# Zeroing the pairs that are not allowed on GpSimd instead of masking the scores on TensorE

## The chip, the cores and the metric

The kernel runs on one core of one Trainium2 chip. The metric is the time of one execution on the device, in microseconds (us), as the median of several runs. Beside it stands one profiled execution, whose trace gives the start and the length of every instruction. The engines are named as in the profile: PE is TensorE (matmuls; PEld its weight loads), DVE is VectorE, ACT is ScalarE, POOL is GpSimd, SP is the queue from which most loads are issued.

## The reference, cut to what matters

The input x has 256 rows of 4096 numbers in float32. The reference normalizes the rows, multiplies them by a 4096 x 16384 matrix, which gives q, k, v and a gate for 32 heads of width 128, runs a stick-breaking attention in each head, multiplies its output by silu(gate) and by a 4096 x 4096 matrix, adds x and normalizes again. What the change touches is the attention of one head:

```python
causal = s_pos[None, :] < t_pos[:, None]
z = jnp.einsum('bhqd,bhkd->bhqk', qb, k, preferred_element_type=jnp.float32) * scale
log_fail = jnp.where(causal, jax.nn.log_sigmoid(-z), 0.0)
suffix = lax.cumsum(log_fail, axis=3, reverse=True) - log_fail
log_a = jax.nn.log_sigmoid(z) + suffix
a = jnp.where(causal, jnp.exp(jnp.where(causal, log_a, 0.0)), 0.0)
return jnp.einsum('bhqk,bhkd->bhqd', a.astype(v.dtype), v)
```

A pair of a query t and a key s is allowed where s < t. Pairs that are not allowed must count nothing in the sum over keys (log_fail is 0) and have no weight (a is 0).

## The kernel before, in words

**The products.** The two big matrices are worked off as 20 units: units 0 to 15 make the projections (two heads each), units 16 to 19 the output. A unit has 16 steps along the 4096 rows of the matrix. The matrix is float32; each tile of it is split by ScalarE into a rounded high part (the casts `wh<-raw`) and by VectorE into the rest (the subtractions `wl<-raw,wh`), and x is split likewise. One product is three matmuls: high by high, high by low, low by high (`mm3`, L813). In units 1 to 15 ten of the 16 steps save one product of eight by sums of blocks: seven products, for which VectorE makes three sums (`sums`, L423) and GpSimd issues two loads that add to what a tile holds (`add_block`, L400). A unit has thus 10 x 7 + 6 x 8 = 118 products. Loads go from SP's queue into 7 buffers `raw`; there are 7 buffers of high parts and 5 of low parts, and TensorE's products follow in a fixed order.

**The order of the work.** `Plan` (L113) lays out the program before it runs. Each piece of work asks for an engine with a cost and a due time; the planner simulates the engines, gives an engine that is free the piece that is due first (`turn`, L229), and emits the instructions in the order of this simulation. Each engine then works off its own list in that order and waits on semaphores where data are not there yet. Costs are formulas by columns (L101 to L110); behind its end a result counts as seen after a tail that depends on the engine: 190 ns for TensorE, 114 for VectorE, 125 for ScalarE, 50 for GpSimd (L122). The issue of a load counts 550 ns on GpSimd (L354). TensorE's pieces of a head (`ten`, L345) ask 400 ns after their input is seen and then go ahead of the next product. Buffers are places in rings (`take`, `give`): `gh` has 4 places and holds the heads' tiles, `att` has one, a bank of PSUM.

**A head.** When a unit's sums are in PSUM, `combine` (L709) puts them together on VectorE and ScalarE into `qk_sb` and `gv_sb`, `gate` (L796) works out silu of the gate, and the two heads follow one after the other while TensorE is in the next unit. `head` (L824) is one chain:

1. TensorE turns q and k (tile `tr`); ScalarE copies them to `qkT`.
2. `scores` (L847): TensorE makes z, 128 keys by 3 x 128 columns. The first 128 columns are the later keys with the later queries, the next 128 the earlier keys with the earlier queries, the last 128 the earlier keys with the later queries. Only the first two squares, the diagonal ones, hold pairs that are not allowed. A third product adds to both squares: an identity (`ident_b`) by a square `off` that holds -3e38 where the key is not before the query, and 0 elsewhere.
3. ScalarE makes ln(1 + exp(-|z|)) in f (L860), VectorE adds max(z, 0) (L867): the softplus. Where z is -3e38 it is 0.
4. ScalarE rounds f to `fh` (L872), VectorE takes the rest `fl` (L873).
5. `scan` (L879): TensorE subtracts from z the sums of f over the keys from each key on, as products with a triangle of -1, and turns the gate's first half.
6. `weights_of` (L897): ScalarE makes a = exp(-relu(-z)). Where z is -3e38 it is 0.
7. `out_of_head` (L909): TensorE multiplies a by v into o and turns the gate's second half; VectorE multiplies o by the gate into `gated`, which GpSimd's queue moves to DRAM at the end of the unit's heads.

The constants come from the start (L619 to L638): GpSimd fills and cuts the triangle and the square `off_f` with affine_select, which keeps an element or replaces it by a fill value, as a linear function of row and column says; VectorE casts them in `constants` (L701). Every instruction that the planner emits has the line L132 in the profile, that of its helper, so the groups are told apart by their tiles.

Of the kernel before, what the change touches and what calls it, by code (L numbers as in the profile page):

```python
# [10 lines left out]
F32 = mybir.dt.float32  # L11
F32R = mybir.dt.float32r
BF16 = mybir.dt.bfloat16
AF = mybir.ActivationFunctionType
ALU = mybir.AluOpType
# [4 lines left out]
P = 128  # L20
# [32 lines left out]
ROWS = 4  # L53
# [47 lines left out]
def vector_ns(n):  # L101
    return 67 + 1.0417 * n


def scalar_ns(n):
    return 98 + n / 1.2


def tensor_ns(n):
    return 0.4167 * n + 8.5 if n > 128 else 109.0  # L110
# [138 lines left out]
def kernel(  # L249
# [10 lines left out]
    nc = Plan(tc)  # L260
# [3 lines left out]
    wp = ctx.enter_context(tc.tile_pool(name="weights", bufs=1))  # L264
# [5 lines left out]
    ap = rooms.enter_context(tc.tile_pool(name="attention", bufs=1))  # L270
# [4 lines left out]
    def minus(out_, full, part):  # L275
        nc.vector.tensor_tensor(out=out_, in0=full, in1=part.bitcast(F32), op=ALU.subtract)
# [34 lines left out]
    for g, (n, k) in enumerate(order):  # L311
        p = parts[n]
        b = p["u"], p["prods"][k][0]
# [12 lines left out]
    def soon(c=4.0):  # L326
        return nc.here + 1e3 * c


    def dve(emit, n, key=None, more=0, **kw):  # L330
        n = n if isinstance(n, tuple) else (n,)
        cost = sum(vector_ns(m) for m in n) + 122 * (len(n) - 1) + more
        return nc.work("vector", cost, emit, soon() if key is None else key, **kw)

    def act(emit, n, key=None, **kw):
        n = n if isinstance(n, tuple) else (n,)
        cost = sum(scalar_ns(m) for m in n) + 100 * (len(n) - 1)
        return nc.work("scalar", cost, emit, soon() if key is None else key, **kw)


    FULL_P, FULL_S = (P,) * 2, (W,) * 2
# [3 lines left out]
    def ten(emit, *n):  # L345
        def others():
            nonlocal since_others
            since_others = 0
            emit()

        return nc.work("tensor", 40 + sum(tensor_ns(m) for m in n), others, nc.here - 1e4, wait=400)
# [262 lines left out]
    for k in range(WARM):  # L614
# [4 lines left out]
    ident = ap.tile([P, P], F32, name="ident")  # L619
    make_identity(tc.nc, ident)  # L620

    nc.rings["gh"][1] += 1
    squares_f = wp.tile([P, 2, P], F32, tag="gh", name="squares_f", bufs=ROWS)
    tri_f, off_f = squares_f[:, 0, :], squares_f[:, 1:2, :]
    nc.gpsimd.memset(tri_f, -1.0)
    nc.gpsimd.affine_select(
        out=tri_f, in_=tri_f, compare_op=ALU.is_ge, fill=0.0, base=0, pattern=[[-1, P]], channel_multiplier=1,
    )

    nc.gpsimd.memset(off_f, -3e38)  # L630
    nc.gpsimd.affine_select(
        out=off_f, in_=off_f, compare_op=ALU.is_ge, fill=0.0, base=0,
        pattern=[[0, 1], [-1, P]], channel_multiplier=1,
    )
    off = ap.tile([P, 1, P], BF16, name="off")
    ident_b = ap.tile([P, P], BF16, name="ident_b")
    neg_tri = ap.tile([P, P], F32R, name="neg_tri")
    neg_one = neg_tri[:, 0:1].broadcast_to([P, P])  # L638

# [61 lines left out]
    def constants():  # L701
        yield nc.until(("used", 0, 1))
        yield dve(lambda: nc.vector.tensor_copy(neg_tri, tri_f), P)
        yield dve(lambda: nc.vector.tensor_copy(off, off_f), P)
        yield dve(lambda: nc.vector.tensor_copy(ident_b, ident), P)
        nc.give("gh")


# [110 lines left out]


    BW = 3 * P
    not_before = off.broadcast_to([P, 2, P])

    def head(u, i):  # L824
        yield nc.take("att", "gh", sooner=True)
        tr = att.tile([P, 2, S], F32, tag="att", name=f"tr{u}_{i}")

        def turn():
            for k in range(2):
                for t in range(NT):  # L830
                    c = k * CW + i * P
                    nc.tensor.transpose(tr[:, k, t * P : (t + 1) * P], st["qk", u][:, t, c : c + P], ident)

        yield ten(turn, P, P, P, P)
        if i == HG - 1:
            nc.give("one")
        qk = wp.tile([P, 2, S], F32, tag="gh", name=f"qkT{u}_{i}", bufs=ROWS)
        yield act(lambda: nc.scalar.copy(qk, tr), 2 * S)
        nc.give("att")
        yield nc.take("att", sooner=True)  # L840
        bank = att.tile([P, W], F32, tag="att", name=f"z{u}_{i}")
        z, gT = bank[:, 0:BW], bank[:, BW:W]

        def turned(to, t):
            nc.tensor.transpose(to, st["gv", u][:, t, i * P : (i + 1) * P], ident)

        def scores():  # L847
            kw = dict(stop=False, skip_group_check=True)
            nc.tensor.matmul(z[:, 0:P], qk[:, 1, P:S], qk[:, 0, P:S], start=True, **kw)
            nc.tensor.matmul(z[:, P:BW], qk[:, 1, 0:P], qk[:, 0, :], start=False, **kw)  # L850
            diagonal = z[:, 0 : 2 * P].rearrange("p (a b) -> p a b", a=2)
            nc.tensor.matmul(diagonal, ident_b, not_before, start=False, **kw)

        yield ten(scores, *FULL_P, *FULL_S, 2 * P)
        nc.give("gh")
        yield nc.take("gh", sooner=True)

        f = wp.tile([P, BW], F32, tag="gh", name=f"f{u}_{i}", bufs=ROWS)

        def soft():  # L860
            nc.scalar.activation(f, z, AF.Abs, scale=scale)
            nc.scalar.activation(f, f, AF.Exp, scale=-1.0)
            nc.scalar.activation(f, f, AF.Ln, bias=1.0)
            nc.scalar.activation(f, f, AF.Copy, scale=1.0 / scale)

        yield act(soft, (BW,) * 4)
        yield dve(  # L867
            lambda: nc.vector.scalar_tensor_tensor(out=f, in0=z, scalar=0.0, in1=f, op0=ALU.max, op1=ALU.add), BW
        )
        yield nc.take("gh", "gh", sooner=True)  # L870
        fh, fl = (wp.tile([P, BW], F32R, tag="gh", name=f"f{k}{u}_{i}", bufs=ROWS) for k in "hl")
        yield act(lambda: nc.scalar.copy(fh, f), BW)  # L872
        yield dve(lambda: minus(fl, f, fh), BW)  # L873
        nc.give("gh")

        if i == 0:
            yield nc.until(("gate", u))

        def scan():  # L879
            kw = dict(start=False, skip_group_check=True)  # L880
            nc.tensor.matmul(z, neg_tri, fh, stop=False, **kw)
            nc.tensor.matmul(z, neg_tri, fl, stop=False, **kw)
            nc.tensor.matmul(z[:, 2 * P : BW], neg_one, fh[:, 0:P], stop=False, **kw)
            nc.tensor.matmul(z[:, 2 * P : BW], neg_one, fl[:, 0:P], stop=True, **kw)
            turned(gT, 0)

        yield ten(scan, BW, BW, P, P, P)
        nc.give("gh", "gh")
        if i == 0:
            yield nc.take("gh", sooner=True)  # L890
            st["o", u] = wp.tile([P, 4, P], F32, tag="gh", name=f"gated{u}", bufs=ROWS)
        gated = st["o", u][:, 2 * i : 2 * i + 2, :].rearrange("p a b -> p (a b)")
        yield nc.take("gh", sooner=True)
        a = wp.tile([P, BW], F32, tag="gh", name=f"a{u}_{i}", bufs=ROWS)


        def weights_of():  # L897
            nc.scalar.activation(a, z, AF.Relu, scale=-scale)
            nc.scalar.activation(a, a, AF.Exp, scale=-1.0)

        yield act(weights_of, (BW, BW))
        yield act(lambda: nc.scalar.copy(gated[:, 0:P], gT), P)
        nc.give("att")
        yield nc.take("att", sooner=True)
        bank2 = att.tile([P, BW], F32, tag="att", name=f"o{u}_{i}")
        o, gT2 = bank2[:, 0:S], bank2[:, S:BW]
        v = lambda t: st["gv", u][:, t, CW + i * P : CW + (i + 1) * P]

        def out_of_head():  # L909
            kw = dict(skip_group_check=True)  # L910
            nc.tensor.matmul(o, v(0), a[:, P:BW], start=True, stop=False, **kw)
            nc.tensor.matmul(o[:, P:S], v(1), a[:, 0:P], start=False, stop=True, **kw)
            turned(gT2, 1)

        yield ten(out_of_head, *FULL_P, *FULL_S, P)
        nc.give("gh")
        if i == HG - 1:
            nc.give("two")
        yield act(lambda: nc.scalar.copy(gated[:, P:S], gT2), P)
        yield dve(lambda: nc.vector.tensor_tensor(out=gated, in0=o, in1=gated, op=ALU.mult), S)  # L920
        nc.give("att")
# [332 lines left out]
    def products():  # L1254
        for g, (n, k) in enumerate(order):
# [18 lines left out]
            nc.here = g * PRODUCT  # L1274

    together(split(KT, "w", HIGHS), split(1, "s", SINGLES), products(), x_stats(), x_factor(), constants())

    def in_turn(works):
# [55 lines left out]
```

## Time and profile before

| What | us |
|---|---|
| median of 3 runs | 1699.45 |
| lowest and highest | 1698.41, 1699.90 |
| the profiled execution's own time | 1698.9 |
| its span, from the first to the last instruction | 1697.1 |
| mean granted TensorE clock, as a share of full speed | 0.997 |
| VectorE: all 128x1024 low parts `wl<-raw,wh`, 813 of 1.22 us | 974.4 |
| GpSimd: 300 issues of adding loads of `w_in` | 258.3 |

The span leaves out what lies before the first and behind the last instruction, 1.8 us here. Busy times of different engines lie beside each other and do not add up. A row of a group gives the engine, the operation, the tile that it writes and those that it reads, the shapes, the count, the busy time, the mean length of one in ns, and the idle time of the engine just before it with what ended it. A row of a timeline gives start and length in us; rows of like instructions that follow each other are one row with a count (x2).

### The profile page before, as it was taken

The numbers are of one execution on the slowest core, as the hardware profiler recorded it, in microseconds if no ns is written. First come the engines' busy times: TensorE is split into PE (matmuls) and PEld (weight loads), VectorE is DVE, ScalarE is ACT, GpSimd is POOL, SyncE is SP. The second block draws the span as 40 slices with busy tenths as digits, with TensorE's granted clock in tenths as the row PEclk, the third lists the DMA queues.
The fourth block names the chain that finished last, engine by engine and source line by source line (L and its number), as shares of the span: only waits on it lengthen the run. The fifth ranks groups of instructions, "written<-read, shape, count | busy, mean of one in ns | idle before, by whom it ended". The sixth has DMA issues, their size and how long they took to land.

```text
span 1697.1 us, 25128 instructions
## 1 busy us (share of the span) xinstructions
PE 1680.2 (99%) x7776; PEld 1417.4 (84%) x7776; DVE 1602.0 (94%) x2025; ACT 1206.7 (71%) x1665; POOL 324.9 (19%) x400
## 2 busy tenths in 40 slices
PE   9999999999999999999999999999999999999997
PEld 7888888888888888888888888888888888888885
DVE  8899999999999999999999999999999978999997
ACT  8986767676767676767676767676868775656654
POOL 0012222121222222222212121212122111212110
PEclk9999999999999999999999999999999999999998
DMA  9978888878787878797978797979797978888895
GB/s 343 332 197 247 232 247 222 252 217 253 215 256 212 256 212 266 199 272 196 276 201 269 198 268 196 272 198 269 204 264 210 300 230 266 245 245 256 246 304 185
DMA packets 248438, 412.77 MB, mean 243 GB/s; under 512 B 28016, under 2 KB 72560, under 8 KB 248304
## 3 DMA queue, kind: packets, MB, share of 16 engines
q1 hardware_dynamic: 194544, 354.24, 62.7%
q0 software_dynamic: 53472, 56.65, 20.0%
q8 instruction: 61, 1.00, 0.2%
q14 instruction: 73, 0.60, 0.1%
q10 hardware_dynamic: 288, 0.28, 0.1%
HBM read 402.93 MB, written 8.13 MB: 242 GB/s over the span
## 4 chain that ended last, share of the span: by engine, by line
PE 94%; DVE 3%; DMA 1%; issue 1%; ACT 1%; SPq 0%; DVEq 0%; ACTq 0%
PE acc L132 89%; PE z L132 3%; PE o L132 1%; DVE wl L132 1%; PE tr L132 1%; DVE h L132 1%; DVE raw L132 0%; ACT wh L132 0%; DMA raw<-in_w_out_dram 0%; DMA raw<-in_w_in_dram 0%; DMA xres<-in_x_dram 0%; SPq L132 0%; ACT sq L132 0%; DVE scalars L132 0%; DVE qk_sb L132 0%
## 5 line engine op out<-in xcount | busy, mean ns | idle before, releaser
L132 ACT CAST wh<-raw 128x1024 fp32r<-128x1024 f32 (+1 forms) x989 | 919.3, 970 | 385.5 <-DVE raw L132 160.9
L132 DVE TENSOR_TENSOR wl<-raw,wh 128x1024 fp32r<-128x1024 f32 (+1 forms) x815 | 975.7, 1220 | 49.3 <-ACT wh L132 23.9
L132 PE MATMUL acc<-wh,sh 128*128 128x512 f32 x2048 | 771.9, 389 | 0.1
L132 PE MATMUL acc<-wh,sl 128*128 128x512 f32 x1898 | 727.1, 383 | 1.8 <-DVE sl L132 1.8
L132 PE MATMUL acc<-wl,sh 128*128 128x512 f32 x1748 | 668.9, 383 | 0.1
L132 PEld LDWEIGHTS acc<-wh,sh 128*128 128x128 f32 x2048 | 384.0, 188 | 77.9 <-DVE qk_sb L132 4.9
L132 POOL DMA_DIRECT2D raw<-in_w_in_dram x300 | 258.3, 947 | 972.2 <-DMA raw<-in_w_in_dram 375.1
L132 PEld LDWEIGHTS acc<-wh,sl 128*128 128x128 f32 x1898 | 356.0, 188 | 66.3 <-DVE sl L132 2.4
L132 PEld LDWEIGHTS acc<-wl,sh 128*128 128x128 f32 x1748 | 328.4, 188 | 55.6 <-DVE wl L132 0.4
L132 DVE TENSOR_TENSOR raw<-raw,raw 128x512 f32<-128x512 f32 x348 | 238.3, 688 | 15.3 <-DMA raw<-in_w_in_dram 11.7
L132 PE MATMUL acc<-wh,oh 128*128 128x512 f32 x512 | 192.4, 383 | 0.0
L132 PE MATMUL acc<-wh,ol 128*128 128x512 f32 x488 | 186.7, 383 | 0.0
L132 PE MATMUL acc<-wl,oh 128*128 128x512 f32 x464 | 177.6, 383 | 1.4 <-DVE wl L132 1.4
L132 DVE TENSOR_TENSOR wh<-raw,wh 128x512 fp32r<-128x512 f32 x174 | 119.7, 688 | 3.3 <-ACT wh L132 2.7
L132 DVE TENSOR_TENSOR raw<-raw 128x512 f32<-128x512 f32 x174 | 119.4, 686 | 0.0
L132 PEld LDWEIGHTS acc<-wh,oh 128*128 128x128 f32 x512 | 96.1, 188 | 17.3
L132 PEld LDWEIGHTS acc<-wh,ol 128*128 128x128 f32 x488 | 91.5, 188 | 16.1
L132 PEld LDWEIGHTS acc<-wl,oh 128*128 128x128 f32 x464 | 87.1, 188 | 17.6 <-DVE wl L132 2.2
L132 POOL DMA_DIRECT2D raw<-in_w_out_dram x48 | 41.5, 984 | 173.8 <-DMA raw<-in_w_out_dram 85.2
L132 ACT ACTIVATE f<-f 128x384 f32<-128x384 f32 x96 | 50.5, 526 | 3.0
L132 POOL DMA_DIRECT2D p<-spill x27 | 17.0, 676 | 89.9 <-DVE ol L132 32.0
L132 DVE SCALAR_TENSOR_TENSOR gv_sb<-acc,scalars,gv_sb 128x512 f32<-128x512 f32 x45 | 33.5, 745 | 0.0
(86 smaller groups left out, 765.7 us busy)
## 6 DMA issues: line engine op xcount, KB each, us to landing
raw<-in_w_in_dram SPq DMA_DIRECT2D x1024, 256.0 KB, 4.5
raw<-in_w_out_dram SPq DMA_DIRECT2D x256, 256.0 KB, 4.5
raw<-in_w_in_dram POOLq DMA_DIRECT2D x300, 128.0 KB, 5.2
p<-spill POOLq DMA_DIRECT2D x27, 256.0 KB, 4.6
raw<-in_w_out_dram POOLq DMA_DIRECT2D x48, 128.0 KB, 5.4
xr<-in_x_dram SPq DMA_DIRECT2D x16, 256.0 KB, 5.3
xres<-in_x_dram SPq DMA_DIRECT2D x16, 256.0 KB, 5.5
out_dram<-h SPq DMA_DIRECT2D x16, 256.0 KB, 2.8
```

Of the source, the lines that this page charges most:

```text
L132: return self.tc.keep_in_program_order(getattr(self.engine, name)(*args, **kw))
```

## The change

The masking product goes, and with it the square `off`, its cut on GpSimd, the identity in bf16 and VectorE's two casts. In its place GpSimd runs affine_select in place on the two diagonal squares (128 x 256 elements) of f, between VectorE's softplus and ScalarE's rounding, and on those of a, between ScalarE's exp and TensorE's product with v. It replaces by 0 what stands at a key that is not before the query. z itself is no longer masked. The planner is told of 500 ns on GpSimd for each select, due like the other steps of the head.

```diff
-    squares_f = wp.tile([P, 2, P], F32, tag="gh", name="squares_f", bufs=ROWS)
-    tri_f, off_f = squares_f[:, 0, :], squares_f[:, 1:2, :]
+    tri_f = wp.tile([P, P], F32, tag="gh", name="tri_f", bufs=ROWS)
     nc.gpsimd.memset(tri_f, -1.0)
...
-    nc.gpsimd.memset(off_f, -3e38)
-    nc.gpsimd.affine_select(
-        out=off_f, in_=off_f, compare_op=ALU.is_ge, fill=0.0, base=0,
-        pattern=[[0, 1], [-1, P]], channel_multiplier=1,
-    )
-    off = ap.tile([P, 1, P], BF16, name="off")
-    ident_b = ap.tile([P, P], BF16, name="ident_b")
...
         yield dve(lambda: nc.vector.tensor_copy(neg_tri, tri_f), P)
-        yield dve(lambda: nc.vector.tensor_copy(off, off_f), P)
-        yield dve(lambda: nc.vector.tensor_copy(ident_b, ident), P)
...
-    not_before = off.broadcast_to([P, 2, P])
+
+    def before(t):
+
+        def cut():
+            blocks = t[:, 0 : 2 * P].rearrange("p (a b) -> p a b", a=2)
+            nc.gpsimd.affine_select(
+                out=blocks, in_=blocks, compare_op=ALU.is_ge, fill=0.0, base=-1, pattern=[[0, 2], [1, P]],
+                channel_multiplier=-1,
+            )
+
+        return nc.work("gpsimd", 500, cut, soon())
...
             nc.tensor.matmul(z[:, P:BW], qk[:, 1, 0:P], qk[:, 0, :], start=False, **kw)
-            diagonal = z[:, 0 : 2 * P].rearrange("p (a b) -> p a b", a=2)
-            nc.tensor.matmul(diagonal, ident_b, not_before, start=False, **kw)
-
-        yield ten(scores, *FULL_P, *FULL_S, 2 * P)
+
+        yield ten(scores, *FULL_P, *FULL_S)
...
             lambda: nc.vector.scalar_tensor_tensor(out=f, in0=z, scalar=0.0, in1=f, op0=ALU.max, op1=ALU.add), BW
         )
+        yield before(f)
...
         yield act(weights_of, (BW, BW))
+        yield before(a)
         yield act(lambda: nc.scalar.copy(gated[:, 0:P], gT), P)
```

## The prediction, made before the changed kernel ran

> **What bounds the kernel now.** I read the page first: the busy shares, the forty slices and the chain that ended last.
>
> ```profile
> PE 1680.2 (99%) x7776; PEld 1417.4 (84%) x7776; DVE 1602.0 (94%) x2025; ACT 1206.7 (71%) x1665; POOL 324.9 (19%) x400
> PE   9999999999999999999999999999999999999997
> DVE  8899999999999999999999999999999978999997
> PE 94%; DVE 3%; DMA 1%; issue 1%; ACT 1%; SPq 0%; DVEq 0%; ACTq 0%
> ```
>
> TensorE bounds: it is busy in every slice and carries 94% of the chain. VectorE is a close second in nearly every slice. GpSimd is idle four fifths of the time, but its queue is not empty: it issues the accumulating loads. So there are two questions. What does TensorE save? And can the other engines, above all VectorE, carry what replaces it without making TensorE wait?
>
> The heads of units 0 to 14 lie in units 1 to 15, all built alike. The view by windows over most of these units gives VectorE's margin.
>
> ```profile
> 173.00:1354.00 1181.00, 1180.91 (x5508) 997.42 (x5507) 1139.62 (x1367) 859.10 (x1143) 249.53 (x297) 1.00 0.83 236
> ```
>
> The columns are length, then busy time and count of PE, PEld, DVE, ACT, POOL. A unit has 118 products of three matmuls and two heads of 19 (tr 4, z 4, mask 1, scan 4, o 4, two gate transposes): 392. So 5508 matmuls are 14.05 units of 84.05 us, in which VectorE is busy 81.1 us and idle 2.95 us. The granted clock is 1.00.
>
> Where that idle time lies, and how far VectorE runs ahead of TensorE, I read in the timeline of one unit (597 to 681 us):
>
> ```profile
> 606.80 1.23 DVE L132 TENSOR_TENSOR wl<-raw,wh 128x1024 fp32r<-128x1024 f32 x1 [0.84 <-ACT wh L132]
> 638.93 0.42 DVE L132 TENSOR_TENSOR gated<-o,gated 128x256 f32<-128x256 f32 x1 [0.16 <-ACT gated L132]
> 655.69 1.22 DVE L132 TENSOR_TENSOR wl<-raw,wh 128x1024 fp32r<-128x1024 f32 x1 [0.32 <-PE acc L132]
> 674.83 1.23 DVE L132 TENSOR_TENSOR wl<-raw,wh 128x1024 fp32r<-128x1024 f32 x1 [0.34 <-ACT qk_sb L132]
> 609.01 2.35 DVE L132 TENSOR_TENSOR wl<-raw,wh 128x1024 fp32r<-128x1024 f32 x2
> 612.29 0.38 PE L132 MATMUL acc<-wh,sh 128*128 128x512 f32 x1
> ```
>
> The heads stand at 600 to 639 us. In that stretch VectorE has one gap worth naming, 0.84 us; the others come later. The lead is thinnest at 612 us: I paired the low parts in order with the parts whose products use them, and the first of the two writes at 609.01 (1.22 us, so done at 610.23) belongs to the product that starts at 612.29. The lead there is 2.06 us, elsewhere in the unit 2 to 10 us. A loss on VectorE is first paid from this lead, then by TensorE.
>
> **What goes.** Per head one bf16 matmul of 256 columns and one weight load, on the engine that bounds.
>
> ```profile
> L132 PE MATMUL z<-off,ident_b 128*128 128x256 bf16 x32 | 8.7, 273 | 0.0
> 602.84 0.27 PE L132 MATMUL z<-off,ident_b 128*128 128x256 bf16 x1
> 602.62 0.10 PEld L132 LDWEIGHTS <-ident_b 128*128 128x128 bf16 x1
> 602.84 0.19 PEld L132 LDWEIGHTS acc<-wh,sh 128*128 128x128 f32 x1
> 602.95 0.19 PEld L132 LDWEIGHTS acc<-wl,sh 128*128 128x128 f32 x1
> ```
>
> The 273 ns are mostly pipeline. A weight load starts with the matmul before it: the next product's second load comes at 602.95, so the mask held the array from 602.84 to 602.95, 0.11 us. Its own load runs under the matmul before. 32 x 0.111 = **3.6 us** saved; the ceiling would be 32 x 0.273 = 8.7. I take 3.6, as the other spacing is overlap. At the start one memset and one select on POOL go, and two casts on VectorE, once 0.46 us at most by this row; I count nothing.
>
> ```profile
> L132 DVE CAST ident_b<-ident 128x128 bf16<-128x128 f32 x1 | 0.2, 230 | 0.0
> ```
>
> **What comes.** 64 selects of 128x256 on GpSimd, two per head, each in the head's chain: VectorE's f, select, ScalarE's fh, VectorE's fl, TensorE's scan; and ScalarE's a, select, TensorE's o. The trace has only smaller ones:
>
> ```profile
> L132 POOL TENSOR_SCALAR_AFFINE_SELECT squares_f<-squares_f 128x128 f32<-128x128 f32 x2 | 0.7, 344 | 0.1
> L132 POOL MEMSET squares_f<- 128x128 f32 x2 | 0.4, 205 | 3.2 <-DVE idle L132 3.2
> L1321 POOL MEMSET const-float32-1.0<- 128x1 f32 x1 | 0.1, 98 | 0.0
> ```
>
> With 98 ns fixed, 344 ns leave 1.92 ns a column, so 256 columns take 0.59 us. The bounds are 0.45 (344 and 128 more columns at the memset's 0.84 ns) and 0.69 (twice 344). The planner counts 0.50 and a tail of 0.05.
>
> Two costs follow. **First, the chains.** What the planner adds it also gives the later steps. Each chain has its own spare time besides, to be read between the end of the producer and the matmul behind it:
>
> ```profile
> 628.99 0.56 DVE L132 SCALAR_TENSOR_TENSOR f<-z,f 128x384 f32<-128x384 f32 x1
> 630.04 0.51 ACT L132 CAST fh<-f 128x384 fp32r<-128x384 f32 x1
> 631.79 0.56 DVE L132 TENSOR_TENSOR fl<-f,fh 128x384 fp32r<-128x384 f32 x1
> 633.65 0.34 PE L132 MATMUL z<-fh,neg_tri 128*128 128x384 f32 x1
> 635.41 0.53 ACT L132 ACTIVATE a<-a 128x384 f32<-128x384 f32 x1
> 637.68 0.70 PE L132 MATMUL o<-a,gv_sb 128*128 128x256 f32 x3
> 615.65 0.53 ACT L132 ACTIVATE a<-a 128x384 f32<-128x384 f32 x1
> 617.63 0.81 PE L132 MATMUL o<-a,gv_sb 128*128 128x256 f32 x4
> ```
>
> The second head's scan has 633.65 - 632.35 = 1.30 us, its o 637.68 - 635.94 = 1.74, the first head's o 617.63 - 616.18 = 1.45. (The first head's scan also waits for the gate and has some 5 us.) With the planner's 0.55, a select may take 1.85, 2.29 and 2.00 us from producer to consumer. It needs 0.59 and two hand-overs. A hand-over is 0.09 us by these rows:
>
> ```profile
> 603.67 1.64 ACT L132 ACTIVATE f<-f 128x384 f32<-128x384 f32 x3
> 605.40 0.55 DVE L132 SCALAR_TENSOR_TENSOR f<-z,f 128x384 f32<-128x384 f32 x1
> 607.20 0.50 ACT L132 CAST fh<-f 128x384 fp32r<-128x384 f32 x1
> ```
>
> That makes 0.77 us, so over 1 us is left at each place and I charge the chains nothing. Behind a late select ScalarE's fh would wait, and the wh casts behind that; at 607.20 fh starts 1.25 us after f ends, so ScalarE covers 0.77 there.
>
> On GpSimd's queue the selects stand among the accumulating loads:
>
> ```profile
> 607.40 1.73 POOL L132 DMA_DIRECT2D raw<-in_w_in_dram  x2 [9.12 <-issue]
> 616.40 1.73 POOL L132 DMA_DIRECT2D raw<-in_w_in_dram  x2 [7.26 <-DVE wl L132]
> DVE raw L132 <- DMA raw<-in_w_in_dram: 11.7, 10, 2.1
> ```
>
> A load held behind a waiting select comes a microsecond or two late. VectorE waited for one only 10 times, 11.7 us in all, so most land early; I count nothing. The other way round, a pair of issues ahead of a select delays it by up to 1.73 us. At 616.40 a pair stands where the first head's a is ready (616.18); the planner knows of the pair at 1.10 us, and the 1.45 us above take the difference.
>
> **Second, VectorE.** The trace has no GpSimd computation beside VectorE's, so what a select costs VectorE is unknown. At least nothing: no instruction is added there. At most the whole select and two hand-overs, 0.77 us (0.87 with the longer select), if one engine keeps the other from the memory, or if VectorE stands at fl until the select's chain is through. A gain is excluded apart from the start's casts. I take 0.68, the select and one hand-over, near the upper end, because VectorE has nothing but TENSOR_TENSORs back to back around three of the four places (0.69 us and 1.23 us rows in every gap between them). The first head's f-select falls into the idle 0.84 us and is free.
>
> The sum per unit: busy 81.1, waits that stay as they do not come from a full buffer (0.84, 0.16, 0.34) 1.34, three selects 2.04, together 84.48 us against 84.05 now: +0.43. The rest of the idle time, 1.6 us, is used up. Over 15 units this is 6.4 us, of which the lead of 2.06 us is spent once before TensorE waits: **+4.4 us**. TensorE's saved 0.11 us a head drops out while VectorE sets the pace; in unit 16, where the last two heads are, the same pairing gives leads of 7 us and more, and it is worth 0.2. Profiled execution 1698.9 us (span 1697.1) + 4.4 = 1703.3; the median of the runs lies 0.55 above the profiled one, so **1704 us**. With 0.77 it is 84.75 a unit and +8.4 us; were only the wait for PE (0.32) absorbed, some 19 us more.
>
> The Trainium skill bears on this one unknown: SBUF — State Buffer, section "Who interferes with whom", says that a VectorE instruction with two SBUF inputs contends with a GpSimd instruction that reads SBUF, and that whichever issues second blocks until the first is through. No row here can show it. By that rule the price is the whole select, and the sum is the one above; without it the sum is that of the next part.
>
> **The rivals.**
>
> *All hidden, faster.* VectorE loses under 0.46 us a select: 3 x 0.46 = 1.38 us a unit, which with the 0.22 us that TensorE saves is just the 1.6 us of idle time. Then TensorE sets the pace and the 3.6 us show: 1698.9 - 3.6 = 1695.3, on the median 1695.9. For it: no instruction is added to VectorE, and the four places are 6 to 13 us apart, so the lead can grow back. Against it: the 0.69 and 1.23 us rows without a gap. The skill has a rule for it too: GPSIMD Engine Reference, "Engine selection", calls one-input work on GpSimd roughly line-rate. An estimate from its 1.2 GHz is 0.21 us for 256 columns; the row of 344 ns for 128 columns speaks against it.
>
> *TensorE waits for the selects.* If a select must wait for VectorE, more than 1.1 us of waiting (1.85 - 0.77) makes the second head's scan late. One VectorE instruction of 1.22 us costs 0.14 us a unit, 2 us in all. Two in a row (2.44 us) cost 1.36 + 1.21 + 0.92 = 3.5 us a unit, 52 us in all: 1748. A select behind a late pair of loads has the same price. I give the case 1707 to 1748 us.
>
> *The new order.* The planner lays out all engines anew. A few products may stand differently around the heads, and the saving may be lost without a new bound: about 1699.
>
> **How the numbers follow.** About 0.2% (1696.0 to 1702.9) is what a measurement of this kernel can tell from no change. Forecast (VectorE pays, 1700 to 1714): 0.44, a quarter of it inside 0.2%. Hidden: 0.28, of which two thirds beyond 0.2%. TensorE waits: 0.20, all slower. New order: 0.08, inside. So faster 0.19, same 0.28, slower 0.53. The range runs from 1694.5, the hidden case with a little more saved, to 1722, the lower part of TensorE's waits; both signs hold weight, and the forecast's own range is 1700 to 1714.
>
> **What would show it.** In the new profile: selects of 0.45 to 0.69 us; per unit, VectorE's idle time gone or its TENSOR_TENSORs longer; PE waits on VectorE's wl at steps 2 and 3 of a unit, growing from unit to unit. If instead DVE idle is as before and PE is 99% busy, the second case holds; if waits of z or o on POOL or fl stand out, the third. The prediction is wrong if VectorE's rows keep their lengths beside the selects and its leads recover within each unit.

## The result: 25 us slower, all of it in one wait

The changed kernel takes 1724.73 us as the median of four runs (1724.02 to 1725.83), against 1699.48 us before; the ratio is 1.0153, with a 95% interval of 1.0140 to 1.0165. The forecast was 1704 us and the range ended at 1722, so the direction was right; the size and the cause were not.

The page of the profile after: busy shares, TensorE's slices, and the chain that ended last by engine and by line.

```profile
span 1722.8 us, 25157 instructions
PE 1682.4 (98%) x7744; PEld 1414.3 (82%) x7744; DVE 1612.5 (94%) x2023; ACT 1209.4 (70%) x1665; POOL 404.6 (23%) x462
PE   9999999999999999999999999999999999999997
PE 79%; DVE 7%; issue 7%; ACT 3%; POOL 3%; DMA 1%; DVEq 0%; SPq 0%; POOLq 0%; ACTq 0%
PE acc L132 75%; POOL a L132 3%; DVE wl L132 2%; PE o L132 2%; PE z L132 2%; DVE gv_sb L132 1%; DVE raw L132 1%; ACT wh L132 1%; ACT f L132 1%; DMA raw<-in_w_in_dram 1%; DVE qk_sb L132 1%; ACT gl L132 1%; DVE h L132 1%; PE tr L132 1%; DVE fl L132 0%
L132 POOL TENSOR_SCALAR_AFFINE_SELECT a<-a 128x256 f32<-128x256 f32 x32 | 56.8, 1776 | 132.7 <-ACT a L132 128.0
L132 POOL TENSOR_SCALAR_AFFINE_SELECT f<-f 128x256 f32<-128x256 f32 x32 | 22.6, 705 | 180.5 <-DVE f L132 124.9
```

The slices tell nothing: 25 us in 1700 do not move a digit. The chain does: TensorE's share falls from 94% to 79%, and a GpSimd group of 32 instructions has 3%. The groups show which: the same instruction with the same shape takes 705 ns on f and 1776 on a. A mean that differs so much for one form asks for the single instructions.

How often and how long TensorE waited for it stands in the view of waits (total, times, longest); the weight loads' row is the same wait seen from PEld.

```profile
PE o L132 <- POOL a L132: 23.1, 14, 2.7
PEld o L132 <- POOL a L132: 29.0, 14, 3.1
```

Fourteen waits, not 32. The timeline of one of them, the first head in the unit that the prediction looked at:

```profile
627.02 0.40 PE L132 MATMUL acc<-wh,sl 128*128 128x512 f32 x1
628.98 0.48 PE L132 MATMUL o<-a,gv_sb 128*128 128x256 f32 x1 [1.56 <-POOL a L132]
```

```profile
625.86 3.06 POOL L132 TENSOR_SCALAR_AFFINE_SELECT a<-a 128x256 f32<-128x256 f32 x1 [6.74 <-ACT a L132]
```

```profile
625.57 0.69 DVE L132 TENSOR_TENSOR raw<-raw,raw 128x512 f32<-128x512 f32 x1
626.17 0.69 DVE L132 TENSOR_TENSOR wh<-raw,wh 128x512 fp32r<-128x512 f32 x1
626.77 1.29 DVE L132 TENSOR_TENSOR raw<-raw,raw 128x512 f32<-128x512 f32 x2
627.97 0.68 DVE L132 TENSOR_TENSOR raw<-raw 128x512 f32<-128x512 f32 x1
628.58 1.43 DVE L132 TENSOR_TENSOR wl<-raw,wh 128x1024 fp32r<-128x1024 f32 x1
```

The select starts when a is ready and ends 3.06 us later. Beside it VectorE runs five instructions back to back, each with two inputs in SBUF and each of its usual length (a `raw<-raw` reads two parts of one tile). The sixth, at 628.58, takes 1.43 us where this form takes 1.22: the select ran in its first part, and 0.2 us is all that VectorE lost. In the first heads this select takes 5.41 us once, 2.90 to 3.13 us thirteen times and 0.50 us twice; in the second heads 0.44 to 1.25 us. The second heads' selects, too, stand beside two-input instructions of VectorE. Some start just before VectorE runs dry; others, such as that at 475.53 (1.11 us), get in at the next boundary between two of them:

```profile
474.55 0.69 DVE L132 TENSOR_TENSOR raw<-raw,raw 128x512 f32<-128x512 f32 x1 [1.19 <-DMA raw<-in_w_in_dram]
475.16 1.22 DVE L132 TENSOR_TENSOR wl<-raw,wh 128x1024 fp32r<-128x1024 f32 x1
476.29 0.89 DVE L132 TENSOR_TENSOR raw<-raw,raw 128x512 f32<-128x512 f32 x1
```

VectorE had stood idle for 1.19 us shortly before. Whether that is what opens the boundary was not tested.

TensorE's next matmul usually starts 0.22 us after the last; here it starts 1.96 us after, and the block's first matmul is 0.1 us longer: its weight load waited as well (the PEld row above). That is 1.84 us a unit lost and, as the experiments show, 0.26 saved with the masks of two heads: 1.58. The distance of VectorE's f in the first heads of two successive units agrees within 0.1 us, in the kernel before (whose row at 605.40 stands above) and in the one after:

```profile
689.46 0.55 DVE L132 SCALAR_TENSOR_TENSOR f<-z,f 128x384 f32<-128x384 f32 x1
```

```profile
615.08 0.55 DVE L132 SCALAR_TENSOR_TENSOR f<-z,f 128x384 f32<-128x384 f32 x1
700.83 0.55 DVE L132 SCALAR_TENSOR_TENSOR f<-z,f 128x384 f32<-128x384 f32 x1
```

This unit takes 85.75 us instead of 84.06, 1.69 more. The first unit with heads loses 3.3 us, the second 0.5, the others about 1.7 each: from the first unit's f to the last one's these are 25.4 of the 25.7 us by which the spans differ.

### The profile page after: what moved, and what is told of

The parts are those of the page before. It is cut to its first block, busy times and chain, and to the rows that moved or that the text cites. A ratio compares the mean times of both kernels' runs of the same rounds, so it can differ in the third digit from the quotient of the medians.

```text
span 1722.8 us, 25157 instructions
## 1 busy us (share of the span) xinstructions
PE 1682.4 (98%) x7744; PEld 1414.3 (82%) x7744; DVE 1612.5 (94%) x2023; ACT 1209.4 (70%) x1665; POOL 404.6 (23%) x462
## 4 chain that ended last, share of the span: by engine, by line
PE 79%; DVE 7%; issue 7%; ACT 3%; POOL 3%; DMA 1%; DVEq 0%; SPq 0%; POOLq 0%; ACTq 0%
PE acc L132 75%; POOL a L132 3%; DVE wl L132 2%; PE o L132 2%; PE z L132 2%; DVE gv_sb L132 1%; DVE raw L132 1%; ACT wh L132 1%; ACT f L132 1%; DMA raw<-in_w_in_dram 1%; DVE qk_sb L132 1%; ACT gl L132 1%; DVE h L132 1%; PE tr L132 1%; DVE fl L132 0%
## 5 line engine op out<-in xcount | busy, mean ns | idle before, releaser
L132 POOL TENSOR_SCALAR_AFFINE_SELECT a<-a 128x256 f32<-128x256 f32 x32 | 56.8, 1776 | 132.7 <-ACT a L132 128.0
L132 POOL TENSOR_SCALAR_AFFINE_SELECT f<-f 128x256 f32<-128x256 f32 x32 | 22.6, 705 | 180.5 <-DVE f L132 124.9
```

Of the source, the lines that this page charges most:

```text
L132: return self.tc.keep_in_program_order(getattr(self.engine, name)(*args, **kw))
```

## The experiments

The theories: **A**, the blocked select: GpSimd's read gets no access to SBUF while VectorE runs instructions with two SBUF inputs back to back, and TensorE waits at o. **B**, as predicted: VectorE pays for each select and falls behind. **C**: GpSimd itself, its queue of load issues or a late start, stretches the instruction. Ratios are to runs of the kernel before on the same chip.

| Kernel | median us | before | ratio, 95% interval |
|---|---|---|---|
| select on f alone | 1695.69 | 1698.54 | 0.9985 (0.9975 to 0.9994) |
| select on a alone | 1724.15 | 1698.54 | 1.0150 (1.0134 to 1.0165) |
| memset in place of the select on a | 1697.76 | 1698.54 | 0.9995 (0.9985 to 1.0004) |
| a cut on VectorE | 1700.75 | 1698.54 | 1.0013 (1.0004 to 1.0023) |
| planner told 3100 ns for a | 1712.59 | 1698.84 | 1.0089 (1.0066 to 1.0112) |
| told 3100 for a and 2500 for f | 1698.01 | 1698.84 | 0.9998 (0.9989 to 1.0008) |
| four small memsets on VectorE | 1698.65 | 1698.84 | 1.0001 (0.9991 to 1.0010) |
| told, memsets for unit 0's heads | 1696.91 | 1698.50 | 0.9989 (0.9980 to 0.9998) |
| told, 6500 for the very first a | 1695.66 | 1698.50 | 0.9982 (0.9973 to 0.9991) |

**One part alone.** Each leaves out one of the two calls.

```diff
-        yield before(a)
```

> The changed kernel without the select on a (a keeps the weights of pairs that are not allowed; that part of the computation is left out). Theory A, the blocked select (GpSimd's select on the first head's a gets no access while VectorE runs instructions with two SBUF inputs back to back, and TensorE waits at o): all of the loss goes and the 3.6 us of the mask show, 1695 to 1698 us, the selects on f staying at 0.4 to 0.7 us. Theory B, VectorE pays for every select, as predicted: half of the loss stays, about 1710 us.

```diff
-        yield before(f)
```

> The changed kernel without the select on f (the softplus of pairs that are not allowed stays in the sums; that part is left out). Theory A: the first head's a-select still takes about 3 us and TensorE waits about 1.9 us a unit at o, 1722 to 1726 us. Theory B: about 1710 us.

Measured: 1695.69 and 1724.15 us. All of the loss belongs to the select on a, and the removed mask is worth 2.9 us with f still cut on GpSimd. Theory B asked for about 1710 from each, and falls. The f-selects are not immune: in this run those of the second heads take longer than the expected 0.4 to 0.7 us,

```profile
376.67 2.47 POOL L132 TENSOR_SCALAR_AFFINE_SELECT f<-f 128x256 f32<-128x256 f32 x1 [1.79 <-DVE f L132]
```

but they end there at the latest, because VectorE's fl waits for them and VectorE stands still:

```profile
377.66 1.22 DVE L132 TENSOR_TENSOR wl<-raw,wh 128x1024 fp32r<-128x1024 f32 x1
379.72 0.56 DVE L132 TENSOR_TENSOR fl<-f,fh 128x384 fp32r<-128x384 f32 x1 [0.85 <-ACT fh L132]
```

VectorE has nothing from 378.87 on, and the select ends at 379.14. Behind the select on a nothing of VectorE waits so soon: its product of o by the gate comes only after the whole row. It does stop VectorE in the end: the 5.41 us of the very first select end in VectorE's idle time before this product.

**Does it block as a reader?** A memset writes the same squares and reads nothing.

```diff
-        yield before(a)
+        yield zeroed(a)   # nc.gpsimd.memset(blocks, 0.0)
```

> The select on a is replaced by a memset of the same 128x256 elements on GpSimd, in the same place of its queue and of the chain; it writes and reads nothing (the weights in the diagonal squares are lost, so this part of the computation differs). Theory A, with reading as what is blocked: every memset takes about 0.3 us, the wait at o goes, 1695 to 1698 us. Theory C, something on GpSimd itself or in its queue (the issue of loads beside it, the late start) stretches the instruction: the first head's memset takes about 3 us too and the time stays at 1722 to 1726 us.

Measured: 1697.76 us. At the same place the memset takes 0.31 us, as everywhere (mean 315 ns):

```profile
364.97 0.31 POOL L132 MEMSET a<- 128x256 f32 x1 [7.23 <-ACT a L132]
L132 POOL MEMSET a<- 128x256 f32 x32 | 10.1, 315 | 130.4 <-ACT a L132 125.4 <-DVE wl L132 5.0
```

Its place in the queue, its start (0.28 us behind that of the first of the same five instructions of VectorE, which wl follows) and its neighbours are those of the select; the reading is gone. Theory C falls for this wait.

**By itself.** A kernel of its own: the select on GpSimd, eight instructions of one kind on VectorE, three passes of each.

```python
vec.tensor_copy(sel, one[:, 0:384])            # the select waits for this
pool.affine_select(out=blocks, in_=blocks, ...)
for op in ops: op(o)                           # pair: tensor_tensor(o, one, two) from SBUF; mixed: one input in PSUM; frompsum: a copy out of PSUM; scaled: twelve tensor_scalar from SBUF; ...
```

> A measurement of the disputed cost by itself; nothing of the reference is computed. GpSimd runs the same select (128x256, on its own tile) while VectorE runs eight instructions of one kind back to back. Theory A: beside instructions with two SBUF inputs (o by one, two) it ends only behind the eighth, after some 5 us; beside instructions with one input in PSUM, or only one input, it takes 0.40 to 0.50 us as with VectorE idle. With one small memset on VectorE behind the third instruction it gets in there, 2.2 us. Where the fourth instruction has to wait for ScalarE (copies of 768 to 2048 columns, 0.8 to 2 us, against 1.9 us for the three before it), it gets in at the fourth for the longest copies, and at the eighth for the shortest. Theory C (GpSimd itself): 0.4 to 0.7 us beside all of them.

One input of VectorE's in PSUM, or a copy out of PSUM: 0.41 us in all six passes, as with VectorE idle. Tensor_scalar from SBUF to SBUF, one input: 0.53, 0.47 and 0.47. Two SBUF inputs gave two answers, apart from one pass of 0.41. GpSimd's rows (pair; four pairs with a small memset behind the third; a fourth that waits for ScalarE's 768, 1792 and 2048 columns, first passes), then VectorE's and ScalarE's of the last two:

```profile
15.46 0.74 POOL L45 TENSOR_SCALAR_AFFINE_SELECT sel_pair<-sel_pair 128x256 f32<-128x256 f32 x1 [4.74 <-DVE sel_pair L45]
71.34 2.00 POOL L45 TENSOR_SCALAR_AFFINE_SELECT sel_gap<-sel_gap 128x256 f32<-128x256 f32 x1 [4.03 <-DVE sel_gap L45]
87.67 5.01 POOL L45 TENSOR_SCALAR_AFFINE_SELECT sel_late<-sel_late 128x256 f32<-128x256 f32 x1 [4.56 <-DVE sel_late L45]
186.65 5.01 POOL L45 TENSOR_SCALAR_AFFINE_SELECT sel_late<-sel_late 128x256 f32<-128x256 f32 x1 [4.55 <-DVE sel_late L45]
203.14 2.00 POOL L45 TENSOR_SCALAR_AFFINE_SELECT sel_late<-sel_late 128x256 f32<-128x256 f32 x1 [4.55 <-DVE sel_late L45]
```

```profile
186.41 1.79 ACT L45 ACTIVATE ready<-one,go_late 128x1792 f32<-128x1792 f32 x1 [3.80 <-DVE go_late L45]
188.31 0.68 DVE L45 TENSOR_TENSOR o<-ready,two 128x512 f32<-128x512 f32 x1
202.90 2.00 ACT L45 ACTIVATE ready<-one,go_late 128x2048 f32<-128x2048 f32 x1 [3.69 <-DVE go_late L45]
204.93 0.75 DVE L45 TENSOR_TENSOR o<-ready,two 128x512 f32<-128x512 f32 x1
```

In the first passes of the last kind VectorE came in full flow, and the select ended behind all eight, after 5.01 us; a memset of one column let it in behind the third instruction. The fourth instruction let it in only where its data came late: ready at 188.20 for a start at 188.31 was early enough to keep it out, ready at 204.90 for 204.93 was not.

The kernel agrees. ScalarE's cast, for which the wl at 628.58 waits, and the a that the select reads:

```profile
627.49 1.04 ACT L132 CAST wh<-raw 128x1024 fp32r<-128x1024 f32 x1 [1.55 <-DVE raw L132]
625.26 0.53 ACT L132 ACTIVATE a<-a 128x384 f32<-128x384 f32 x1
```

The cast ends at 628.53, 0.05 us before wl starts, and all thirteen selects of about 3 us end at such a wl. With the select on f alone, a cast that ended 0.06 us before VectorE's next instruction (377.00 for 377.06) left the select out. Lateness is not the whole rule: in the last run below VectorE's instruction at 280.54 depended on a matmul that ended at 280.50, and the select stayed out there.

The expectation was wrong for the kind pair: the select got in behind one instruction, 0.74 us (0.85 in the first pass), and so it did in nearly all second and third passes of the other kinds with two SBUF inputs. In these second and third passes VectorE's first small instruction reads what the select before it wrote, and a gap of 0.03 us follows it (14.94 to 14.97 us in pair's second), where the passes of 5.01 us have none; pair's first pass has none either. What opens the next boundary there, the runs do not show.

**The cut on VectorE.**

```diff
-        yield before(a)
+        yield times(a)   # nc.vector.tensor_tensor(out=blocks, in0=blocks, in1=kept_pairs, op=ALU.mult)
```

> The cut of a is moved to VectorE, as a product in place with a square of 1 and 0 (128x256, about 0.42 us, 32 of them); the cut of f stays on GpSimd. Theory A: TensorE no longer waits at o; VectorE has 0.84 us a unit more, which its idle 2.95 us a unit holds: 1695 to 1700 us. If VectorE's time were what binds (theory B): above 1705 us.

Measured: 1700.75 us, 0.75 above the expected upper end and 2.2 above before. The products take 0.42 us each; TensorE's wait at o is gone, but its weight loads now wait longer for VectorE's qk_sb, the kernel before first:

```profile
PEld acc L132 <- DVE qk_sb L132: 4.9, 14, 0.5
```

```profile
PEld acc L132 <- DVE qk_sb L132: 8.8, 14, 1.2
```

So VectorE's time is not free either: 0.84 us a unit more can be seen in the time. That this wait is the whole difference is not shown.

**Telling the planner.**

```diff
-        return nc.work("gpsimd", 500, cut, soon())
+        return nc.work("gpsimd", cost, cut, soon())
...
+        yield before(a, 3100)
```

> The changed kernel, but the planner is told of 3100 ns for the select on a, not 500, so that it puts more products ahead of o. Theory A: the select still takes up to 3 us, but TensorE has products to do meanwhile; the wait at o goes, 1695 to 1698 us. If the loss were VectorE's (theory B): 1710 us or more.

Measured: 1712.59 us, and the expectation was wrong. After the first two the first heads no longer wait. But with everything moved, the second heads' select falls in five of the units into a denser stretch of VectorE:

```profile
726.54 6.20 POOL L132 TENSOR_SCALAR_AFFINE_SELECT a<-a 128x256 f32<-128x256 f32 x1 [1.87 <-ACT a L132]
```

```profile
732.80 0.48 PE L132 MATMUL o<-a,gv_sb 128*128 128x256 f32 x1 [1.61 <-POOL a L132]
```

In all TensorE waits at o seven times, 11.2 us, and the very first select takes 7.22 us. The length of a select is not its own: it is that of whatever VectorE has in a row. With f's select at 2500 as well, the places move once more:

> As the run before, and 2500 ns for the select on f, so that ScalarE's fh and VectorE's fl are put later too. Theory A: 1695 to 1697 us, TensorE waiting nowhere in the heads.

Measured: 1698.01 us. Most units take 83.8 us, about 0.26 less than before; what is lost lies in unit 1, where the very first select on a takes 5.92 us and TensorE waits.

**Letting it in.**

```diff
+        nc.start(pause())   # four nc.vector.memset(idle_col[:, k : k + 1], 0.0)
         yield before(a)
```

> The changed kernel with four memsets of one column on VectorE put beside each select on a (some 0.06 us each, 0.25 us a head). Theory A: an instruction without a second SBUF input lets the select in; the first head's select takes about 1 us instead of 3.1 and the wait at o goes, 1696 to 1703 us. If instructions of VectorE had no part in it: 1724 us.

Measured: 1698.65 us. The select at the place of the 3 us takes 0.48 (0.48 to 0.73 in the first heads of units 2 to 15, 1.34 in unit 1); VectorE's row is the same five instructions and wl, with a memset at the lengthened one:

```profile
366.29 0.48 POOL L132 TENSOR_SCALAR_AFFINE_SELECT a<-a 128x256 f32<-128x256 f32 x1 [7.83 <-ACT a L132]
```

```profile
366.43 0.88 DVE L132 TENSOR_TENSOR wh<-raw,wh 128x512 fp32r<-128x512 f32 x1
366.45 0.06 DVE L132 MEMSET idle_col<- 128x1 f32 x1
```

Four instructions of 60 ns a head, with no SBUF input, take away 26 us. Theory A asked for this; B and C have no reason for it. The mask's 3 us do not show here: a unit takes about 84.04 us, as before the change.

**Both together, as a better kernel.** The first cuts a and f with told costs from unit 1's heads on, and pauses in unit 0's; the second tells 6500 ns for the very first a, and its calls are those of the diff (in the first, a has 500 and the memsets in unit 0).

```diff
+        yield before(f, 2500 if u else 500)
...
+        yield before(a, 3100 if u else 6500 - 5000 * i)
```

> As the run with both costs told (3100 ns for the select on a, 2500 for that on f), except for the heads of unit 0, where the select on a took 5.9 us and TensorE waited: there the costs stay at 500 and the four small memsets on VectorE let the select in. Theory A: unit 1 comes back from 86.9 us to about 83.2, the other units stay at 83.8, and the 3.6 us that the mask cost show: 1694 to 1696 us, faster than both kernels. If the unit-1 loss has another cause: 1698 us as before.

> The same without the memsets: the planner is told of 6500 ns for the select on a of the very first head, 1500 for the second, and of 500 for their f. Theory A: 1694 to 1697 us; the long wait on GpSimd is still there, but TensorE has products meanwhile.

Measured: 1696.91 and 1695.66 us; the second is faster than both kernels, by 0.18% (0.09 to 0.27%) against the one before, the first by 0.11% (0.02 to 0.20%), above its expected 1694 to 1696. In the second the select on a is as slow as ever, and TensorE does not wait for it:

```profile
363.49 3.07 POOL L132 TENSOR_SCALAR_AFFINE_SELECT a<-a 128x256 f32<-128x256 f32 x1 [7.58 <-ACT a L132]
```

```profile
368.63 0.38 PE L132 MATMUL acc<-wh,sl 128*128 128x512 f32 x1
368.85 0.38 PE L132 MATMUL o<-a,gv_sb 128*128 128x256 f32 x1
```

## Why the prediction was wrong, point by point

- **What goes: 3.6 us.** Right. The kernel with the select on f alone is 2.9 us faster, the one with 6500 told 2.8, and units without a wait are 0.26 us shorter, 0.13 a head against the 0.11 read from the weight loads.
- **The select's length: 0.59 us, bounds 0.45 and 0.69.** With VectorE out of the way it takes 0.40 to 0.42, below the lower bound. It decided nothing.
- **The chains: "I charge the chains nothing".** This step failed. I gave the select its own length and two hand-overs, 0.77 us, and it took 3.1. The room was smaller, too: not 2.00 us at the first head's o but 1.45, from a's end at 625.79 to 627.24, where TensorE was free (0.22 us behind its last start at 627.02). The 0.55 that the planner was to add did not come there. The 0.77 would have fitted all the same. In the sum I treated the contact of the two engines as a price that VectorE pays; in the chain I left it out.
- **VectorE pays 0.68 us a select, +4.4 us.** Failed too, on the other side. VectorE loses about 0.2 us where it meets a select; its busy time grows by 10.5 us in all (1602.0 to 1612.5), about 0.16 a select, and its leads recover: paired as in the prediction, the thinnest lead of that unit is 2.18 us, from 621.04 to 623.22, where it was 2.06:

```profile
619.82 1.22 DVE L132 TENSOR_TENSOR wl<-raw,wh 128x1024 fp32r<-128x1024 f32 x1
```

```profile
623.22 0.38 PE L132 MATMUL acc<-wh,sh 128*128 128x512 f32 x1
```

  Who waits was the wrong way round: the busy engine goes on, and the idle one waits.
- **The rival that TensorE waits for the selects** had the right mechanism, with 0.20, and 1707 to 1748 us hold the result. That is partly luck: the 1707 follows from no number there, as one VectorE instruction, 2 us in all, would give 1702 at most. Its place was wrong: it began with the second head's scan, which VectorE's own wait for fl protects. The first head's o came in only with two of VectorE's instructions in a row, at 1.21 us a unit; it was five, and 1.84. The stretch was there to be read in the timeline of before, around the first head's a, ready at 616.18:

```profile
615.89 0.69 DVE L132 TENSOR_TENSOR raw<-raw,raw 128x512 f32<-128x512 f32 x1
616.49 0.69 DVE L132 TENSOR_TENSOR wh<-raw,wh 128x512 fp32r<-128x512 f32 x1
617.10 1.29 DVE L132 TENSOR_TENSOR raw<-raw,raw 128x512 f32<-128x512 f32 x2
618.30 0.69 DVE L132 TENSOR_TENSOR raw<-raw 128x512 f32<-128x512 f32 x1
618.90 1.22 DVE L132 TENSOR_TENSOR wl<-raw,wh 128x1024 fp32r<-128x1024 f32 x1
```

Five instructions without a gap, then wl: the very ones that held the select after the change.
- **The Trainium skill** (SBUF — State Buffer, "Who interferes with whom") has the pair of instructions right: only the select, which reads, was held, and the memset was not. That the second to issue blocks until the first is through was the ground for my one-sided price; the runs show that the select can stay blocked through several instructions.
- **The range** ended 2.7 us too low: it took in only the lower part of that rival's span.

## What to carry to other kernels

An idle engine is not a free engine: what counts is whether it can reach its data while the busy one works. Before a step moves to GpSimd, look at what VectorE runs beside it, and take the longest unbroken row of two-input SBUF instructions as the delay at worst, not the step's own length; whether VectorE soon waits for the result decides if that delay ends by itself. Where the order is planned by costs, plan with that delay, or put a small instruction with no second SBUF input into VectorE's row.

## What the runs showed of the hardware that was not expected

- A GpSimd select of 0.41 us that reads SBUF took up to 7.22 us beside unbroken two-input SBUF instructions of VectorE, and 5.01 us beside eight of them alone; a memset of the same size took 0.31 us.
- In full flow it was let in at an instruction whose data came late, ready from ScalarE 0.03 to 0.05 us before its start and not 0.06 or 0.11, and at a memset; a matmul that ended 0.04 us before did not let it in. VectorE's instruction at that place was 0.1 to 0.2 us longer.
- In other passes with the same eight instructions it got in behind a single one (0.74 us). What makes the difference stays open.
- Beside tensor_scalar instructions from SBUF to SBUF the same select took 0.47 to 0.53 us, beside instructions with one input in PSUM 0.41.
